# The values of a recurrent mixer leave the projection's front and follow beside the first group's preparation and inversion

## The chip, the cores and the metric

One core of one Trainium2 chip. The metric is the device time of one execution in microseconds (us). The kernel before took 2694.9 us (median of three runs, 2692.5 to 2695.86).

## What is computed

The reference is a trunk of two layers on 256 tokens of width 2048, in float32. Its core for each layer:

```python
mod = (jnp.einsum('bd,de->be', cond, w_ada[l]) + b_ada[l]).reshape(B, N_MOD, 1, D_MODEL)
sh_m, sc_m, gt_m, sh_f, sc_f, gt_f = [mod[:, i] for i in range(N_MOD)]
u = x * (1 + sc_m) + sh_m
proj = u @ w_in[l]                                   # 4896 columns
y_attn = sliding_window_attention(q, k, v, attn_sinks[l], cos, sin)
y_rwkv, v_first = rwkv7_group(proj[..., ATTN_COLS:], ...)
mix = jnp.concatenate([y_attn, y_rwkv], axis=-1) @ w_out[l]
x = layer_norm(DEEPNORM_ALPHA * x + gt_m * mix, ln1_w[l], ln1_b[l])
# then u again with sh_f, sc_f; SwiGLU with 5632 hidden columns; layer_norm
```

Inside `rwkv7_group` the projected columns are 1024 each of r, k and v and 288 low-rank ones (decay, a and gate). Each is mixed with the token before it. From the low-rank ones come the decays w, the rate a and the gate g. In layer 1, v is moved toward layer 0's v (`v_first`) by a gate that is itself computed from v: `v = v + (v_first - v) * sigmoid(v0 + (v @ v1) @ v2)`. Then a state of 64x64 for each of 16 heads runs over the tokens:

```python
S = S * w_t + (S @ a_t) b_t^T + v_t k_t^T     # a = -kk, b = kk * a
out_t = S @ r_t
```

## The kernel before

**Projections.** Weights stream through a pool. `steps` (L363) loads 1024 columns' worth of a weight (`raw`, four buffers, L372), splits them into a rounded part `hi` (ScalarE, L380) and the rest `lo` (VectorE, L381), and each block is three matmuls: hi with the rounded activations, hi with their rest, lo with the rounded ones. `stream` (L402, L403, L405) has tokens on the output's partitions; `tstream` (L414, L415, L416) has the weight's columns there, 128 columns by 256 tokens a matmul. A k-tile is 128 rows of the weight; there are 16. All loads are issued by SyncE (SP) in one order.

**adaLN.** The scales and shifts come from 12 x 2048 columns of `w_ada` a layer, summed by VectorE over 16 rows of k-tiles (L306 for the first scale and shift of layer 0, beside the front; L257 for all others, in the background: `pump()` after each weight step and `adv()` in some places run the next of them). TensorE transposes the sums (L277) and ScalarE adds them up (L281).

**Front.** `front` (L463) runs as soon as parts of the modulated input u are there (`make_u`, L354 to L361). In layer 0 the parts have 4, 4, 2, 4 and 2 k-tiles, and each waits for its part of the first scale and shift. For each part it streams 288 low-rank columns and the 1024 columns of v, and in layer 0 (`ahead`) also 384 of the 512 columns of r and k of the first group: 256 of r, 128 of k. Four accumulators hold v, and in layer 0 a bank that the small products otherwise use holds r.

**Mixer.** `mixer` (L490) first mixes the low-rank columns and all of v with the token before (`shift_mix`, L454, L455); layer 0 stores v, layer 1 loads it and computes the value residual (L523 to L547). The recurrent heads go in four groups of four heads (two pairs), the tokens in four chunks of 64. A string, `ORDER`, one for each layer, gives the order in which the program is written; a scheduler of the framework then sets each engine's order from it. A letter with a group's number stands for:

- D, `decays` (L598 to L625): decays and rates from the low-rank columns; at its end the values are transposed to tokens on partitions (vt, L620).
- R, `project` (L576): r and k of a group. For group 0 of layer 0 only the 128 columns of k that the front left.
- A, `prepare` (L627 to L721): norms (ssb L644, rb L654), the products inside a chunk (aa L681, masked to am L684, stored to DRAM for the inversion L686), the values' product with them (ax L692), at L699, kb L710, and the bonus (bnb L718, bv L720).
- I, `invert` (L723): the inverse of each chunk's unit triangular matrix. Its 16x16 diagonal blocks come back from DRAM (L727), GpSimd (POOL) solves them in 15 steps of two operations (L733, L735), the result goes over DRAM again (L738, L741), and two levels of products follow on TensorE (m, L749 and L756, with VectorE's ytr L745 and yx L752 between).
- C, `recur` (ta L769, tk L775, uv L780, mr L784 and L791, ob, db): the states through the four chunks. E, `close`: normalisation and gate. Q: a third of attention's columns. X changes a pool; a, b, c and w, z are attention and the output projection.

What matters for the order: D, A, I, C of a group follow each other over several engines and DRAM, and the streamed projections R and Q of others are TensorE's work in between.

Of the kernel before, what the change touches and what calls it, by code (L numbers as in the profile page):

```python
# [10 lines left out]
F32 = mybir.dt.float32  # L11
# [8 lines left out]
P = 128  # L20
D = 2048
T = 256
L = 2
KT = D // P
# [4 lines left out]
RW = 1024  # L29
# [12 lines left out]
    "D0 R0 A0 D1 I0 R1 C0 E0 Q1 A1 I1 D2 R2 A2 Q0 D3 C1 R3 E1 I2 A3 X Q2 a0 a1 b0 C2 a2 b1 c0 E2 a3 c1 I3 b2 b3 c2 c3 w0 C3 w1 w2 E3 z0 z1 z2 z3 w3",  # L42
    "D0 R0 A0 D1 R1 I0 C0 Q2 E0 A1 I1 D2 R2 A2 D3 Q1 C1 R3 E1 A3 I2 Q0 X a0 a1 b0 b1 c0 C2 I3 a2 b2 E2 a3 c1 b3 c2 c3 w0 C3 z0 w1 w2 E3 z1 z2 z3 w3",
# [24 lines left out]
def hybrid_trunk_kernel(  # L68
# [19 lines left out]
    turn = [0, 1]  # L88

    def bank(name="mb", tag="mb"):  # L90

        if tag == "cb":
            return ps.tile([P, 512], F32, tag="cb", name=name)
        t = f"m{turn[0]}"
        turn[0] ^= turn[1]
        return ps.tile([P, 512], F32, tag=t, name=name, bufs=1)
# [366 lines left out]
    def front(l, us, feeds, ahead=False):  # L463

        lb = [bank("lb", "cb") for _ in range(2)]
        vb = [acc_ps.tile([P, 512], F32, tag="acc", name="acc") for _ in range(4)]
        lblocks = [(0, 128, lb[0][:, 0:T], True, False), (128, 128, lb[0][:, T:2 * T], False, True),
                   (256, 32, lb[1][0:32, 0:T], not ahead, not ahead)]
        vblocks = [((2 * q + i) * P, P, vb[q][:, i * T:(i + 1) * T], i == 0, i == 1) for q in range(4) for i in range(2)]
        rk = None  # L470
        if ahead:
            b = ps.tile([P, 512], F32, tag="m1", name="rk0", bufs=1)
            turn[:] = 0, 0
            rk = [[b[:, 0:T], b[:, T:2 * T]], [lb[1][:, T:2 * T], None]]
            rblocks = [(0, P, rk[0][0], True, False), (P, P, rk[1][0], True, True), (2 * P, P, rk[0][1], False, True)]
            wrk = w_in[l][:, R0:R0 + 2 * RW].rearrange("(k p) (s n) -> p k s n", p=P, s=2)

            def rk_cols(rv, k0, m):
                return [(rv[:, :, 0:T], wrk[:, k0:k0 + m, 0, 0:T]), (rv[:, :, T:T + P], wrk[:, k0:k0 + m, 1, 0:P])]
        for kts, _ in feeds:  # L480
            fl = dict(first=kts[0] == 0, last=kts[-1] == KT - 1)
            if ahead and kts[0] == 0:
                tstream(rk_cols, T + P, kts, us, rblocks, **fl)
            tstream(cols(w_in[l], LORA0, 288), 288, kts, us, lblocks, **fl)
            if ahead and kts[0] > 0:
                tstream(rk_cols, T + P, kts, us, rblocks, **fl)
            tstream(cols(w_in[l], R0 + 2 * RW, RW), RW, kts, us, vblocks, **fl)
        return lb, vb, rk

    def mixer(l, us, mixp, feeds):  # L490
# [6 lines left out]
        lb, vb, rk = feeds  # L497
        x0 = {}
        if rk:
            for i, s in ((0, 1), (0, 0), (1, 0)):  # L500
                x0[i, s] = pa.tile([P, T], F32, tag=("t_xr", "t_xk")[s], name="x0", bufs=(2, 4)[s])
                shift_mix(l, x0[i, s], rk[i][s], 8 * s + i)
            turn[1] = 1

# [15 lines left out]
        for p in range(NPAIR):  # L520
            shift_mix(l, vx[:, p, :], vb[p // 2][:, p % 2 * T:(p % 2 + 1) * T], 16 + p)
            if l == 0:
                dma(vfirst[p], vx[:, p, :])  # L523
        if l > 0:
# [7 lines left out]
            for p2 in range(4):  # L532
# [3 lines left out]
                for i in range(2):  # L536
                    p = 2 * p2 + i
                    PE.matmul(b[:, i * T:(i + 1) * T], lhsT=v2t[64:96, i * P:(i + 1) * P], rhs=hv, start=True, stop=True)
                for i in range(2):
                    p = 2 * p2 + i  # L540
                    gt = pa.tile([P, T], F32, tag="t_tha", name="gt", bufs=4)
                    S.activation(gt, b[:, i * T:(i + 1) * T], AF.Tanh, scale=0.5, bias=drv(l, "v0h", p))
                    vf = pa.tile([P, T], F32, tag="t_e2", name="vf", bufs=4)
# [6 lines left out]
        left = ["R0", "R1", "R2", "R3", "Q0", "Q1", "Q2"]  # L550
# [19 lines left out]
        wrk = w_in[l][:, R0:R0 + 2 * RW].rearrange("(k p) (s n) -> p k s n", p=P, s=2)  # L570
# [5 lines left out]
        def project(g):  # L576
            if g == 0 and rk:
                b = acc_ps.tile([P, 512], F32, tag="acc", name="acc")
                c0 = R0 + RW + P
                tstream(cols(w_in[l], c0, P), P, list(range(KT)), us, [(0, P, b[:, T:2 * T], True, True)])  # L580
                return [None, b]
            bk = [acc_ps.tile([P, 512], F32, tag="acc", name="acc") for _ in I2]

            def rk_cols(rv, k0, m):
                return [(rv[:, :, s * 256:(s + 1) * 256], wrk[:, k0:k0 + m, s, g * 256:(g + 1) * 256]) for s in range(2)]
            tstream(rk_cols, 512, list(range(KT)), us,
                    [(s * 256 + i * P, P, bk[i][:, s * T:(s + 1) * T], s == 0, s == 1) for i in I2 for s in range(2)])
            return bk

        def decays(g):  # L590
# [26 lines left out]
            vt_ = bank("vt")  # L617
            for cc in range(NCH):
                for i in I2:
                    PE.matmul(vt_[KH[i], cc * P:(cc + 1) * P], lhsT=vx[:, 2 * g + i, cc * CH:(cc + 1) * CH], rhs=cent,  # L620
                              start=True, stop=True)
            for i in I2:
                st[i]["uv"] = uv = pb.tile([P, NCH, P], F32, tag="uv", name="uv", bufs=4)
                S.copy(uv[KH[i]].rearrange("p c s -> p (c s)"), vt_[KH[i]])
            return st  # L625

        def prepare(g, st, bk):  # L627

            nscr = dram.tile([4 * NCH, CH + 1, CH], F32, tag="nscr", name="nscr", bufs=3)
            for i in I2:  # L630
                s_, p = st[i], 2 * g + i
                for s, nm in ((1, "xk"), (0, "xr")):
                    if g == 0 and (i, s) in x0:
                        s_[nm] = x0[i, s]
                    else:
                        s_[nm] = pa.tile([P, T], F32, tag=f"t_{nm}", name=nm, bufs=(2, 4)[s])
                        shift_mix(l, s_[nm], bk[i][:, s * T:(s + 1) * T], 8 * s + p)
# [50 lines left out]
            ax = bank("ax")  # L688
            for cc in range(NCH):
                for h in range(2):  # L690
                    for i in I2:
                        PE.matmul(ax[BH[i], cc * P + h * CH:cc * P + (h + 1) * CH], lhsT=st[i]["am"][h][KH[i], cc, 0:CH],  # L692
                                  rhs=st[i]["uv"][KH[i], cc, h * CH:(h + 1) * CH], start=True, stop=True)
            for i in I2:
                S.copy(st[i]["uv"][BH[i]].rearrange("p c s -> p (c s)"), ax[BH[i]])
# [6 lines left out]
            for i in I2:  # L702
# [9 lines left out]
                S.copy(bkt.rearrange("p c s -> p (c s)"), kb[:, 0:(NCH - 1) * P])  # L712
            bnb = bank("bnb")
# [7 lines left out]
            return nscr  # L721
# [286 lines left out]
        st, bks, nscr = {}, {}, {}  # L1008
# [6 lines left out]
        for op in ORDER[l].split():  # L1015
# [7 lines left out]
            elif op[0] == "A":  # L1023
                nscr[n] = prepare(n, st[n], bks[n])
            elif op[0] == "I":
# [260 lines left out]
    with tc.tile_pool(name="pro", bufs=1) as pp:  # L1286
# [27 lines left out]
        feeds = front(0, us, parts(), ahead=True)  # L1314
# [37 lines left out]
```

## Time and profile before

| what | value |
|---|---|
| median of three runs | 2694.9 us |
| the profiled execution | 2694.28 us |
| its span in the trace | 2692.6 us |
| mean granted TensorE clock | 0.965 |
| TensorE (PE) busy | 2501.1 us, 93% |
| VectorE (DVE) busy | 1841.0 us, 68% |
| ScalarE (ACT) busy | 1188.3 us, 44% |
| GpSimd (POOL) busy | 135.0 us, 5% |
| moved by DMA | 637.49 MB, 237 GB/s on average |

In a row of groups stand: line, engine, operation, out<-in, shapes and count; then the busy time and the mean duration in ns; then the idle time of the engine ahead of these instructions, and who ended it. In a row of the timeline stand the start, the duration, and in brackets the idle time ahead, and who ended it. Matmuls overlap in the pipeline, so their cost in a row of them is the distance between starts. In the table of stretches, each engine's busy time and its number of instructions follow the stretch's length; then come the granted clock, the DMA share and GB/s.

### The profile page before, as it was taken

What the parts mean: (1) busy time and instruction counts of PE and PEld (TensorE: products, weight loads), DVE (VectorE), ACT (ScalarE), POOL (GpSimd) and SP (SyncE); (2) the same over time, 40 slices, a digit from 0 to 9 for tenths busy, and PEclk for the clock granted to TensorE, in tenths of its full rate; (3) what the DMA queues carried; (4) which work ended last, traced back from release to release, by engine and by line L of the source; (5) the groups of instructions that cost most, each with busy time, mean ns of one, the idle gap of its engine ahead of it and who ended that gap; (6) DMA issues with size and microseconds to landing.
All of it is one profiled execution on the core that took longest, in us unless ns stands there. A gap on an engine that the chain in (4) does not pass through costs nothing.

```text
span 2692.6 us, 41752 instructions
## 1 busy us (share of the span) xinstructions
PE 2501.1 (93%) x15325; PEld 2093.1 (78%) x15325; DVE 1841.0 (68%) x2469; ACT 1188.3 (44%) x2029; POOL 135.0 (5%) x355
## 2 busy tenths in 40 slices
PE   3788998788999999999999999979899999999997
PEld 2687886567888888888889877867688888888887
DVE  6866767979877777777788677555764545545456
ACT  2364452435444444444445544534444444344442
POOL 1002112000000000000000022110000000000000
PEclk9789998899999999999999999989999999999999
DMA  9968668688998888889878586424756656666654
GB/s 315 381 188 253 198 191 238 180 317 296 353 330 309 297 303 312 293 295 308 308 263 304 174 259 188 117 72 144 253 172 188 190 186 196 195 189 189 193 188 149
DMA packets 351999, 637.49 MB, mean 237 GB/s; under 512 B 75894, under 2 KB 142898, under 8 KB 350258
## 3 DMA queue, kind: packets, MB, share of 16 engines
q1 hardware_dynamic: 351794, 634.82, 71.6%
q8 instruction: 120, 1.97, 0.3%
q14 instruction: 85, 0.70, 0.1%
HBM read 622.08 MB, written 12.62 MB: 236 GB/s over the span
## 4 chain that ended last, share of the span: by engine, by line
PE 68%; DMA 8%; DVE 6%; ACT 2%; issue 1%; POOL 1%; SPq 0%; DVEq 0%; POOLq 0%; ACTq 0%
PE acc L403 19%; PE acc L402 19%; PE acc L405 19%; DMA ast<-in_w_ada_dram 3%; DVE aacc L257 2%; PE acc L414 2%; PE acc L415 2%; PE acc L416 2%; DVE lo L381 1%; DMA raw<-in_w_gate_up_dram 1%; PE mb L1225 1%; DMA raw<-in_w_out_dram 1%; DMA yf<-yd 1%; PE mb L277 1%; ACT pr L947 0%
## 5 line engine op out<-in xcount | busy, mean ns | idle before, releaser
L380 ACT CAST hi<-raw 128x1024 fp32r<-128x1024 f32 (+2 forms) x728 | 758.5, 1044 | 1110.8 <-PE acc L405 833.1
L381 DVE TENSOR_TENSOR lo<-raw,hi 128x1024 fp32r<-128x1024 f32 (+2 forms) x728 | 880.2, 1212 | 519.8 <-PE acc L403 347.1
L403 PE MATMUL acc<-lo,u 128*128 128x512 f32 x1568 | 513.4, 395 | 11.9 <-DVE lo L381 11.8
L405 PE MATMUL acc<-hi,u 128*128 128x512 f32 x1568 | 505.8, 391 | 0.0
L257 DVE SCALAR_TENSOR_TENSOR aacc<-ast,cond,aacc 128x1024 f32<-128x1024 f32 x300 | 384.1, 1280 | 127.8 <-DMA ast<-in_w_ada_dram 126.6
L402 PE MATMUL acc<-hi,u 128*128 128x512 f32 x1568 | 457.2, 393 | 0.9 <-ACT u L360 0.5
L403 PEld LDWEIGHTS acc<-lo,u 128*128 128x128 f32 x1568 | 293.8, 189 | 76.4 <-DVE lo L381 16.2
L402 PEld LDWEIGHTS acc<-hi,u 128*128 128x128 f32 x1568 | 294.9, 188 | 63.4 <-ACT sg L1218 0.9
L405 PEld LDWEIGHTS acc<-hi,u 128*128 128x128 f32 x1568 | 295.2, 188 | 61.8 <-issue 0.5
L403 PE MATMUL acc<-lo,ht 128*128 128x512 f32 (+1 forms) x720 | 243.6, 377 | 3.0 <-DVE lo L381 2.9
L405 PE MATMUL acc<-hi,ht 128*128 128x512 f32 (+1 forms) x720 | 242.2, 375 | 0.0
L414 PE MATMUL acc<-u,hi 128*128 128x256 f32 x720 | 206.1, 293 | 14.0 <-ACT hi L380 14.0
L402 PE MATMUL acc<-hi,ht 128*128 128x512 f32 (+1 forms) x720 | 217.0, 376 | 0.0
L415 PE MATMUL acc<-u,hi 128*128 128x256 f32 x720 | 204.5, 291 | 0.0
L416 PE MATMUL acc<-u,lo 128*128 128x256 f32 x720 | 193.1, 294 | 7.1 <-DVE lo L381 7.1
L403 PEld LDWEIGHTS acc<-lo,ht 128*128 128x128 f32 x720 | 135.0, 188 | 29.3 <-DVE lo L381 5.6
L414 PEld LDWEIGHTS acc<-u,hi 128*128 128x128 f32 x720 | 141.9, 197 | 19.3 <-ACT hi L380 14.9
L405 PEld LDWEIGHTS acc<-hi,ht 128*128 128x128 f32 x720 | 135.6, 188 | 24.2
L402 PEld LDWEIGHTS acc<-hi,ht 128*128 128x128 f32 x720 | 134.8, 188 | 24.4
L415 PEld LDWEIGHTS acc<-u,hi 128*128 128x128 f32 x720 | 141.7, 197 | 2.6 <-issue 1.6
L416 PEld LDWEIGHTS acc<-u,lo 128*128 128x128 f32 x720 | 133.8, 197 | 11.6 <-DVE lo L381 9.0
L1067 POOL TENSOR_TENSOR brs<-brs,mhalf 128x1 f32<-128x1 f32 x8 | 7.6, 955 | 1698.7 <-DVE brs L1066 772.1
(349 smaller groups left out, 2901.1 us busy)
## 6 DMA issues: line engine op xcount, KB each, us to landing
ast<-in_w_ada_dram SPq DMA_DIRECT2D x368, 512.0 KB
raw<-in_w_gate_up_dram SPq DMA_DIRECT2D x704, 256.0 KB
raw<-in_w_down_dram SPq DMA_DIRECT2D x176, 512.0 KB
raw<-in_w_in_dram SPq DMA_DIRECT2D x82, 512.0 KB
raw<-in_w_out_dram SPq DMA_DIRECT2D x64, 512.0 KB
raw<-in_w_in_dram SPq DMA_DIRECT2D x120, 256.0 KB
ast<-in_w_ada_dram SPq DMA_DIRECT2D x32, 256.0 KB
lnw<-in_ln_w_dram SPq DMA_DIRECT2D x4, 1024.0 KB
```

What stands on the lines that cost most here:

```text
L257: ins = V.scalar_tensor_tensor(acc, t, cond[:, j:j + 1], acc, ALU.mult, ALU.add)
L277: PE.transpose(b[:, i * P:(i + 1) * P], blocks[q + i], ident)
L380: S.copy(h, fl)
L381: ins = V.tensor_tensor(r, fl, h.bitcast(F32), ALU.subtract)
L402: PE.matmul(bt, lhsT=xh, rhs=hi[:, c0:c0 + w], start=st, stop=False)
L403: PE.matmul(bt, lhsT=xh, rhs=lo[:, c0:c0 + w], start=False, stop=False)
L405: PE.matmul(banks[t][q][:, 0:w], lhsT=xl, rhs=hi[:, c0:c0 + w], start=False, stop=sp_)
L414: PE.matmul(bt, lhsT=hi[:, c0:c0 + w], rhs=xh, start=st and opens, stop=False)
L415: PE.matmul(bt, lhsT=hi[:, c0:c0 + w], rhs=xl, start=False, stop=False)
L416: PE.matmul(bt, lhsT=lo[:, c0:c0 + w], rhs=xh, start=False, stop=sp_ and closes)
L1067: G.tensor_tensor(rs[:, 0:1], rs[:, 0:1], mhalf[:, 0:1], ALU.pow)
L1225: PE.transpose(b[:, i * T + t * P:i * T + (t + 1) * P], hh[t][:, (2 * k2 + i) * P:(2 * k2 + i + 1) * P], ident)
```

## The change

The front streams, for each part, the 288 low-rank columns and then the 512 columns of r and k of group 0, in both layers, into two accumulators (`rk_stream`, shared with `project`). The values are streamed by a new step V in two halves of 512 columns each, with their own two accumulators, token mixing and store; in layer 1 the residual follows the second half. What needs the values is taken out of D and A into a new step U, `join`: vt, ax, and the bonus. R0 is gone. The two ORDER strings get V and U; the extra r and k columns' special bank and its handling go. The number of streamed matmuls and the bytes loaded stay the same.

```diff
 ORDER = (
-    "D0 R0 A0 D1 I0 R1 C0 E0 Q1 A1 I1 D2 R2 A2 Q0 D3 C1 R3 E1 I2 A3 X Q2 a0 a1 b0 C2 a2 b1 c0 E2 a3 c1 I3 b2 b3 c2 c3 w0 C3 w1 w2 E3 z0 z1 z2 z3 w3",
-    "D0 R0 A0 D1 R1 I0 C0 Q2 E0 A1 I1 D2 R2 A2 D3 Q1 C1 R3 E1 A3 I2 Q0 X a0 a1 b0 b1 c0 C2 I3 a2 b2 E2 a3 c1 b3 c2 c3 w0 C3 z0 w1 w2 E3 z1 z2 z3 w3",
+    "D0 A0 V0 I0 V1 U0 D1 R1 C0 E0 A1 U1 I1 Q1 D2 R2 A2 U2 D3 C1 R3 E1 I2 Q0 A3 U3 X Q2 a0 a1 b0 C2 a2 b1 c0 E2 a3 c1 I3 b2 b3 c2 c3 w0 C3 w1 w2 E3 z0 z1 z2 z3 w3",
+    "D0 A0 I0 V0 V1 U0 D1 R1 C0 Q2 E0 A1 U1 I1 D2 R2 A2 U2 D3 Q1 C1 R3 E1 A3 U3 I2 Q0 X a0 a1 b0 b1 c0 C2 I3 a2 b2 E2 a3 c1 b3 c2 c3 w0 C3 z0 w1 w2 E3 z1 z2 z3 w3",
 )
...
-    def front(l, us, feeds, ahead=False):
+    def rk_stream(l, g, bk, kts, us, first=True, last=True):
+
+        wrk = w_in[l][:, R0:R0 + 2 * RW].rearrange("(k p) (s n) -> p k s n", p=P, s=2)
...
+        tstream(rk_cols, 512, kts, us,
+                [(s * 256 + i * P, P, bk[i][:, s * T:(s + 1) * T], s == 0, s == 1) for i in range(2) for s in range(2)],
+                first, last)
+
+    def front(l, us, feeds):
...
-        vb = [acc_ps.tile([P, 512], F32, tag="acc", name="acc") for _ in range(4)]
+        bk = [acc_ps.tile([P, 512], F32, tag="acc", name="acc") for _ in range(2)]
...
         for kts, _ in feeds:
             fl = dict(first=kts[0] == 0, last=kts[-1] == KT - 1)
-            if ahead and kts[0] == 0:
-                tstream(rk_cols, T + P, kts, us, rblocks, **fl)
             tstream(cols(w_in[l], LORA0, 288), 288, kts, us, lblocks, **fl)
-            if ahead and kts[0] > 0:
-                tstream(rk_cols, T + P, kts, us, rblocks, **fl)
-            tstream(cols(w_in[l], R0 + 2 * RW, RW), RW, kts, us, vblocks, **fl)
-        return lb, vb, rk
+            rk_stream(l, 0, bk, kts, us, **fl)
+        return lb, bk
...
-        for p in range(NPAIR):
-            shift_mix(l, vx[:, p, :], vb[p // 2][:, p % 2 * T:(p % 2 + 1) * T], 16 + p)
-            if l == 0:
-                dma(vfirst[p], vx[:, p, :])
-        if l > 0:
+
+        def values(half):
+
+            vb = [acc_ps.tile([P, 512], F32, tag="acc", name="acc") for _ in range(2)]
+            tstream(cols(w_in[l], R0 + 2 * RW + half * 512, 512), 512, list(range(KT)), us,
+                    [((2 * q + i) * P, P, vb[q][:, i * T:(i + 1) * T], i == 0, i == 1) for q in range(2) for i in range(2)])
+            for j in range(4):
+                p = 4 * half + j
+                shift_mix(l, vx[:, p, :], vb[j // 2][:, j % 2 * T:(j % 2 + 1) * T], 16 + p)
+                if l == 0:
+                    dma(vfirst[p], vx[:, p, :])
+            if l == 0 or half == 0:
+                return
...
+        def join(g, st):
+
+            vt_ = bank("vt")
...
+            ax = bank("ax")
...
             bnb = bank("bnb")
```

The loops of `join` are those that stood in `decays` and `prepare`, word for word.

**What moves, in three places.** First SP, the end of layer 0's front: before, from its last but two adaLN loads on (`ast`; `raw` is a piece of a weight, 128 partitions by its columns).

```order
L372 DMA raw<-in_w_in_dram 128x2x256
L372 DMA raw<-in_w_in_dram 128x2x128
L301 DMA ast<-in_w_ada_dram 128x2x256 x2
L372 DMA raw<-in_w_in_dram 128x1024 x4
L372 DMA raw<-in_w_in_dram 128x2x288
L372 DMA raw<-in_w_in_dram 128x2x256
L372 DMA raw<-in_w_in_dram 128x2x128
L372 DMA raw<-in_w_in_dram 128x1024 x2
```

And the same place after.

```order
L301 DMA ast<-in_w_ada_dram 128x2x256 x4
L372 DMA raw<-in_w_in_dram 128x2x288
L301 DMA ast<-in_w_ada_dram 128x2x256 x2
L372 DMA raw<-in_w_in_dram 128x2x256 x2
L301 DMA ast<-in_w_ada_dram 128x2x256 x10
L372 DMA raw<-in_w_in_dram 128x2x512 x4
L824 DMA g2a<-in_rwkv_g_dram 128x256
```

Behind the last adaLN load stood the front's weights of the last k-tiles; now all of the front's stand ahead of it, and behind it come the values' first weights (2x512).

Second TensorE, where the first product of layer 0's first inversion (m, 64x64) stands: before, amid `stream`ed projections of attention and group 1's decays (ab).

```order
L403 MATMUL acc<-lo,u 128x512
L405 MATMUL acc<-hi,u 128x512
L402 MATMUL acc<-hi,u 128x512
L599 MATMUL ab<-xwa,w2a_1931 128x256 x2
L402 MATMUL acc<-hi,u 128x512
L749 MATMUL m_2036<-ytr,am 64x64 x16
L403 MATMUL acc<-lo,u 128x512
```

And after.

```order
L415 MATMUL acc<-u,hi 128x256
L695 MATMUL ax<-uv,am 64x64
L416 MATMUL acc<-u,lo 128x256 x2
L695 MATMUL ax<-uv,am 64x64 x8
L734 MATMUL m_1693<-ytr,am 64x64 x16
L695 MATMUL ax<-uv,am 64x64 x7
L704 MATMUL bnb<-xr,bones 128x256
```

The inversion's first product now stands among the values' and the next group's `tstream` (128x256) and the join (ax, bnb), and no longer among attention's projections.

Third TensorE, the last preparation of layer 1: before.

```order
L405 MATMUL acc<-hi,u 128x512
L402 MATMUL acc<-hi,u 128x512
L692 MATMUL ax<-uv,am 64x64 x16
L699 MATMUL at<-ident,ar 64x128 x6
L756 MATMUL m_16858<-tm,yx 64x64 x16
L403 MATMUL acc<-lo,u 128x512
L405 MATMUL acc<-hi,u 128x512
L402 MATMUL acc<-hi,u 128x512
L710 MATMUL kb<-de,bkc 128x128 x3
```

And after.

```order
L655 MATMUL aa<-ar,bkc 128x128 x8
L665 MATMUL at<-ident,ar 64x128 x6
L676 MATMUL kb<-de,bkc 128x128 x6
L686 MATMUL vt<-cent,vx 64x128 x8
L843 MATMUL oc<-ident,sq 128x128 x4
L695 MATMUL ax<-uv,am 64x64 x16
L704 MATMUL bnb<-xr,bones 128x256
L734 MATMUL m_16788<-ytr,am 64x64 x16
L704 MATMUL bnb<-xr,bones 128x256
L741 MATMUL m_16807<-tm,yx 64x64 x16
L734 MATMUL m_16827<-ytr,am 64x64 x16
L891 MATMUL acc<-ident,qr 128x128 x6
```

Before, streamed matmuls (128x512) stood among these products; after, none stands behind the second aa of the last group.

More of the change, by code (lines that the diff above doesn't have):

```diff
@@ L576, in project @@
         def project(g):
[L577 to L581, printed above, removed]
             bk = [acc_ps.tile([P, 512], F32, tag="acc", name="acc") for _ in I2]
[L584 to L587, printed above, removed]
+            rk_stream(l, g, bk, list(range(KT)), us)
             return bk
@@ L616, in decays @@
                 S.activation(e2, lw, AF.Exp, scale=-1.0)
[L617 to L624, printed above, removed]
             return st
```

73 lines of the change are left out of this document (32 added, 41 removed).

## The prediction

> **What bounds the kernel now.** I read the page first: the engine totals, then the forty slices.
>
> ```profile
> span 2692.6 us, 41752 instructions
> PE 2501.1 (93%) x15325; PEld 2093.1 (78%) x15325; DVE 1841.0 (68%) x2469; ACT 1188.3 (44%) x2029; POOL 135.0 (5%) x355
> PE   3788998788999999999999999979899999999997
> ```
>
> TensorE is busy for 93% of the span, so whoever wants to gain must take away TensorE's idle time or its work. The slices show where it idles: at the start, in slices 7 and 8, and in slice 27. The change touches each layer's front and the recurrent mixer behind it, so the next view is the table of stretches: from 40 us to the front's end at about 178 us, layer 0's mixer while it has projections to stream (to 424), and layer 1's front and mixer (1402 to 1661). The columns are PE, weight load, DVE, ACT and POOL busy, the granted clock, the DMA share and GB/s.
>
> ```profile
> 40.00:140.00 100.00, 70.75 (x466) 65.93 (x466) 82.72 (x116) 34.11 (x82) 0.00 (x0) 0.85 1.04 365
> 140.00:178.00 38.00, 35.27 (x268) 33.91 (x270) 22.41 (x34) 21.97 (x43) 0.85 (x3) 0.91 0.51 149
> 178.00:424.00 246.00, 232.65 (x2233) 199.35 (x2230) 179.31 (x272) 123.44 (x247) 41.65 (x103) 0.97 0.71 218
> 1402.00:1479.00 77.00, 71.09 (x562) 68.42 (x560) 62.21 (x89) 42.51 (x67) 1.83 (x4) 0.96 0.79 268
> 1479.00:1661.00 182.00, 168.20 (x1452) 143.24 (x1451) 131.18 (x203) 91.21 (x192) 32.93 (x69) 0.95 0.70 212
> ```
>
> The first 140 us of layer 0 are set by the transfers: their share is 1.04 at 365 GB/s while TensorE has gaps. From 140 on TensorE finishes what the transfers brought late. From 178 on it is TensorE that sets the time, with 246 - 232.65 = 13.35 us of idle time up to 424. Layer 1's front and mixer hold 5.9 and 13.8 us. So in layer 0 a matmul in the front may stand beside transfers for nothing; one in the mixer costs its own time.
>
> **Layer 0's front against its mixer.** The groups of streamed matmuls up to 178 us:
>
> ```profile
> L414 PE MATMUL acc<-u,hi 128*128 128x256 f32 x128 | 37.5, 309 | 14.0 <-ACT hi L380 14.0
> L414 PE MATMUL lb<-u,hi 128*128 128x256 f32 (+1 forms) x64 | 18.4, 318 | 3.7 <-ACT u L360 3.7
> L414 PE MATMUL rk<-u,hi 128*128 128x256 f32 x32 | 10.1, 316 | 1.1 <-ACT u L360 1.1
> 190.05 0.28 PE L415 MATMUL acc<-u,hi 128*128 128x256 f32 x1
> 190.17 0.28 PE L416 MATMUL acc<-u,lo 128*128 128x256 f32 x1
> ```
>
> Each of the three lines of the split has as many: the trace holds 128 + 64 + 32 = 224 per line, 672 in all, or 42 per k-tile (24 values, 9 low-rank, 9 of r and k). One starts every 0.12 us. Behind the front stand another 16 x 3 = 48 for the last k columns. After, the front has 9 + 12 = 21 per k-tile, 336 in all, and 384 of the values stand in the mixer. The 48 are gone, so 384 - 48 = 336 matmuls, 336 x 0.12 = 40.3 us, move from the front to the stretch that TensorE sets. That is +40.3.
>
> What the front gives back: its last modulated input, u, is ready at 147.15 us, behind the last of the adaLN sums on DVE.
>
> ```profile
> 142.87 3.11 DVE L306 SCALAR_TENSOR_TENSOR aacc<-ast,cond,aacc 128x512 f32<-128x512 f32 x4
> 146.73 0.42 DVE L361 TENSOR_TENSOR u<-uf,u 128x256 fp32r<-128x256 f32 x1 [0.41 <-ACT u L360]
> 177.34 0.28 PE L416 MATMUL acc<-u,lo 128*128 128x256 f32 x1
> ```
>
> From there to 177.6 are 30.5 us, which is 6 k-tiles x 42 x 0.12 = 30.2. After, the same six hold 21 each: 15.1 us, so -15.1. And the adaLN loads stand behind fewer weights. Before, the front's raw columns are 1696 x 2048 x 4 = 13.9 MB, of which 3.83 MB (by the shapes of the SP order shown with the change) are issued behind the last adaLN load, so 10.06 MB stand ahead. After, all 800 columns, 6.55 MB, stand ahead. The difference, 3.5 MB at 365 GB/s, is 9.6 us. The front ends 24.7 us earlier (at most 30, if the weights that SP holds back for lack of buffers count too; at least 21, if DVE, 82.72 of 100 us busy, is what held the sums). So this term is 40.3 - 24.7 = **+15.6** (+9 to +19). The front gives back less than the mixer takes, because most of what it loses was hidden beside transfers.
>
> **The front's end.** TensorE waits there for the decays of group 0:
>
> ```profile
> 180.63 0.48 PE L620 MATMUL vt<-cent,vx 128*64 128x128 f32 x2 [1.94 <-ACT lw L605]
> 181.70 0.48 PE L644 MATMUL ssb<-bones,kkn 128*64 128x2 f32 x3 [0.59 <-ACT tha L607]
> 185.26 0.41 PE L414 MATMUL acc<-u,hi 128*128 128x256 f32 x1
> 185.47 0.41 PE L415 MATMUL acc<-u,hi 128*128 128x256 f32 x1
> 1481.38 1.92 PE L530 MATMUL mb<-vx,v1t 128*32 128x256 f32 x4 [2.17 <-DVE vx L455]
> ```
>
> After, the first half of the values stands there with its weights loaded, and vt comes much later. The two waits go, 2.53 us, and the slow steps after them (0.21 against 0.12 us, for some 16 matmuls) cost 1.4: **-3.9** (0 if the values' first scale or weight comes late). In layer 1 the wait of the value residual, 2.17 us, and a like restart (1.4 by layer 0's) go the same way: **-3.5** (0 to -4), since the residual then stands behind the second half, with projections to stream.
>
> **The inversions.** With group 0, TensorE's last product of the preparation (aa) leads over DVE, a DMA round trip and POOL's small triangular solve to the first product of the inversion (m). POOL's first and last row give the length of a solve, here of groups 0 and 1 of layer 0; PE's rows are those at the ends of group 0's chain, and two of layer 1 that wait for DVE.
>
> ```profile
> 215.15 1.49 PE L681 MATMUL aa<-ar,bkc 64*128 64x128 f32 x16
> 254.79 1.44 PE L749 MATMUL m<-ytr,am 64*64 64x64 f32 x22 [6.70 <-DVE ytr L745]
> 1571.48 0.50 PE L403 MATMUL acc<-lo,u 128*128 128x512 f32 x1 [2.20 <-DVE lo L381]
> 1655.39 0.80 PE L403 MATMUL acc<-lo,u 128*128 128x512 f32 x1 [5.32 <-DVE lo L381]
> ```
>
> And POOL's, with the row of DVE beside its second step ahead of them:
>
> ```profile
> 227.54 1.23 DVE L381 TENSOR_TENSOR lo<-raw,hi 128x1024 fp32r<-128x1024 f32 x1
> ```
>
> ```profile
> 226.98 0.72 POOL L733 TENSOR_TENSOR tmp<-nb,ttl 128x15 f32<-128x15 f32 x1 [41.32 <-DMA nb<-nscr]
> 227.78 1.07 POOL L735 TENSOR_TENSOR ttl<-ttl,tmp 128x15 f32<-128x15 f32 x1
> 245.44 0.22 POOL L735 TENSOR_TENSOR ttl<-ttl,tmp 128x8 f32<-128x8 f32 x1
> 297.36 0.21 POOL L733 TENSOR_TENSOR tmp<-nb,ttl 128x15 f32<-128x15 f32 x1 [48.18 <-DMA nb<-nscr]
> 297.65 0.21 POOL L735 TENSOR_TENSOR ttl<-ttl,tmp 128x15 f32<-128x15 f32 x1
> 308.18 0.22 POOL L735 TENSOR_TENSOR ttl<-ttl,tmp 128x8 f32<-128x8 f32 x1
> ```
>
> Group 0's solve takes 18.7 us, its chain from aa's end (216.6) to m 38.2, and m waits 6.70. Group 1's solve, the same steps, takes 11.0, so its chain would be 30.5. In the order after, the work that TensorE has between aa and m is 197, 105, 193 and 134 streamed matmuls and small ones of 4 to 14 us: about 28, 27, 29 and 25 us in the first two inversions of layers 0 and 1. Whether that covers depends on how long the solve gets. With 30.5 everywhere the waits are 2.5, 3.5, 1.5 and 5.5, 13 in all; with 38.2 they are 10, 11, 9 and 13, 43 in all; 6.7 now. I take the first inversion as it is (10) and the short chain in the other three (10.5), which is 13.8 more, and set off the two waits for DVE in layer 1 (2.20 and 5.32) that would fall into them: **+6** (0 to +24).
>
> POOL's step takes 0.21 us at 297.65 and 1.07 at 227.78, beside a DVE row with two inputs (the split lo takes from the weights the cast hi). The Trainium skill ("SBUF — State Buffer", section "SBUF: two separate sides") says that DVE and GpSimd share a port pair under an exclusive lock, held for a whole instruction, when the DVE one has two SBUF inputs. This trace agrees (0.21 against 1.07). By that rule more DVE splits beside each solve mean the long chain in each, and 2742 as in the rival of the long solves below.
>
> **The late mixer.** Layer 0 streams its last projection at 423.6; what follows is the last preparation, bare:
>
> ```profile
> 423.60:443.20 19.60, 15.14 (x186) 12.19 (x185) 11.97 (x16) 5.97 (x16) 3.44 (x14) 0.84 0.86 250
> 428.08 0.44 PE L692 MATMUL ax<-uv,am 64*64 64x64 f32 x6 [1.72 <-DVE am L684]
> 439.29 0.63 PE L277 MATMUL mb<-ident,aacc 128*128 128x128 f32 x4 [2.58 <-DVE aacc L257]
> 1760.07 0.40 PE L405 MATMUL acc<-hi,u 128*128 128x512 f32 x1
> ```
>
> It idles 4.46 us. After, two query projections stand later, beside it: **-4** (-8 to 0). In layer 1 the projections run until 1760 and cover the last preparation today. In the order after, groups 1 to 3 stand later among the streamed matmuls, and the second half of the last preparation, its join and the products of group 2's inversion stand behind the last of them. The same stretch bare cost 4.46 in layer 0: **+5** (0 to +15, if the waits of that inversion are as long as group 0's 6.70 above, twice).
>
> The values' 8.4 MB of weights now stand beside the background adaLN loads; the mixer's share is 0.71, so there is room on average, and I take **+2** (0 to +5) for moments of both. The inversion split in two (what needs the values in a step of its own) adds no instruction.
>
> **Sum.** 15.6 - 3.9 - 3.5 + 6 - 4 + 5 + 2 = +17.2. The profiled execution took 2694.28 us, 1.7 over its span and 0.6 under the median of 2694.9; with it 2694.3 + 17.2 = 2711.5. The bounds above, added as independent (the root of the sum of squares), give -11 and +22, 2700 to 2733 for this case.
>
> **Rivals.** *A wash.* The inversions are covered, the late mixer of layer 1 shows nothing and no transfers crowd: 2694.3 + 15.6 - 3.9 - 3.5 - 4 = 2698.5. For it: group 1 waits for nothing today. Against: less work stands between than today in three of four.
>
> *Faster: the moved matmuls fill idle time.* If the values, free to be streamed at any time, take the place of TensorE's 13.35 idle us in layer 0's mixer and the 13.8 in layer 1's, these fall off instead of the single waits: 2694.3 + 15.6 - 13.35 - 13.8 = 2682.8, 11.5 under now. Against: the idle time is many waits under 3 us for a split or a scale, which a streamed matmul has too. It decides if the stretch behind the front holds under 3 us of idle.
>
> *Long solves.* All four solves take the 18.7 us of group 0: waits of 43 instead of 6.7, +36.4 in place of +6, and 2742. It decides where DVE's splits and adaLN sums fall on most of POOL's steps. For it: the values' splits now stand beside the solves. Against: group 1's 11.0, with DVE working too. (The Trainium skill's lock of the port pair, "SBUF — State Buffer", would lead here.)
>
> *The values' weights starve.* If their stream came slower than 0.12 us a matmul, the front would give its 24.7 and the mixer take more than 40.3; the DMA share of 0.71 says no, and I count it within the range.
>
> **Numbers.** The forecast 0.52, the wash 0.17, the faster case 0.19, the long solves 0.12. Of this kernel a measurement tells about 0.2%, 5.4 us, from no change: the wash lies within that, with some of the forecast's lower end, and a little of the wash is below it. Faster 0.20, the same 0.18, slower 0.62. The range takes in the faster case and the forecast's upper end and leaves out most of the long solves: 2681 to 2736.
>
> **What would show it.** In the profile after, the last streamed matmul of layer 0's front should end near 153 us (177.6 now), and the stretch from there to the last streamed projection should be some 40 us longer. Waits of 2 to 10 us should stand at the first m of the first two inversions. The last preparation in layer 1 should be bare, in layer 0 covered. I am wrong if the front ends before 140, if TensorE's idle time in the two mixers falls by over 15 us, or if POOL's solves last 18 us throughout.

## The result and the profile after

The changed kernel takes 2731.6 us (median of four runs, 2724.1 to 2736.5) beside 2693.7 us before: a ratio of 1.0136, 95% interval 1.0121 to 1.0151. It is slower by 38 us, where 17 were forecast. The profiled execution took 2730.35 us, with a span of 2728.6, 36.0 over that of before.

The page of after, its totals and the slices that answer to those shown:

```profile
span 2728.6 us, 41739 instructions
PE 2507.5 (92%) x15325; PEld 2094.2 (77%) x15325; DVE 1843.4 (68%) x2467; ACT 1186.0 (43%) x2027; POOL 142.1 (5%) x355
PE   2598989788999999999999999978999999999998
```

TensorE's work is the same within 6.4 us; 29.6 of the 36.0 us are idle time. The table of stretches says where. To compare, both kernels are cut at the same streamed matmuls: the end of layer 0's front, the mixer's last streamed projection, the end of the output projection, of the feed-forward part (FFN), and the same three for layer 1. First before, then after, with the columns as in the prediction:

```profile
0.00:177.60 177.60, 108.97 (x743) 101.42 (x743) 129.72 (x189) 62.59 (x144) 10.63 (x66) 0.89 0.90 307
177.60:423.60 246.00, 232.65 (x2232) 199.34 (x2231) 179.38 (x272) 123.53 (x247) 41.65 (x103) 0.97 0.71 218
423.60:635.80 212.20, 175.69 (x1253) 137.28 (x1252) 171.10 (x319) 85.90 (x234) 16.63 (x36) 0.88 0.79 259
635.80:1399.00 763.20, 749.01 (x3478) 619.74 (x3479) 592.60 (x597) 348.85 (x537) 2.45 (x2) 0.99 0.89 307
1399.00:1760.50 361.50, 341.79 (x3116) 298.76 (x3115) 251.84 (x389) 180.99 (x350) 55.09 (x138) 0.97 0.65 201
1760.50:1935.20 174.70, 155.40 (x1104) 121.31 (x1102) 110.57 (x262) 74.74 (x166) 4.66 (x7) 0.91 0.46 151
```

```profile
0.00:151.00 151.00, 66.38 (x409) 58.66 (x409) 109.80 (x167) 43.16 (x119) 10.59 (x66) 0.82 0.92 312
151.00:459.00 308.00, 286.06 (x2637) 248.40 (x2637) 219.55 (x311) 142.82 (x286) 55.58 (x107) 0.97 0.72 221
459.00:660.80 201.80, 168.26 (x1182) 132.54 (x1182) 162.93 (x309) 82.89 (x218) 15.34 (x33) 0.86 0.77 259
660.80:1433.30 772.50, 751.22 (x3478) 619.46 (x3479) 591.19 (x595) 349.30 (x537) 1.06 (x2) 0.99 0.88 302
1433.30:1776.40 343.10, 327.99 (x2865) 288.09 (x2865) 234.23 (x366) 175.81 (x339) 41.01 (x107) 0.97 0.66 201
1776.40:1972.10 195.70, 171.75 (x1357) 133.08 (x1356) 120.16 (x279) 80.69 (x178) 14.77 (x38) 0.92 0.42 136
```

The differences are -26.6, +62.0, -10.4 and +9.3 in layer 0, -18.4 and +21.0 in layer 1, and -0.9 in layer 1's FFN. Layer 0 up to its FFN's end loses 34.3 us, layer 1's two stretches together 2.6. The front is where the trade shows: 42.6 us of TensorE's busy time left it, and it became 26.6 shorter, so its idle time rose from 68.6 to 84.6 us. In the mixer behind it 53.4 us of busy time and 8.6 of idle time came on top.

The front's end, and the two waits at the first inversions in layer 0:

```profile
132.19 0.42 DVE L361 TENSOR_TENSOR u<-uf,u 128x256 fp32r<-128x256 f32 x1
...
140.27 1.53 DVE L306 SCALAR_TENSOR_TENSOR aacc<-ast,cond,aacc 128x512 f32<-128x512 f32 x2
...
145.98 0.42 DVE L361 TENSOR_TENSOR u<-uf,u 128x256 fp32r<-128x256 f32 x1 [1.32 <-ACT u L360]
146.89 0.42 DVE L361 TENSOR_TENSOR u<-uf,u 128x256 fp32r<-128x256 f32 x1 [0.49 <-ACT u L360]
...
220.04 0.69 PE L734 MATMUL m<-ytr,am 64*64 64x64 f32 x8 [6.94 <-DVE ytr L730]
...
321.44 0.59 PE L734 MATMUL m<-ytr,am 64*64 64x64 f32 x6 [5.31 <-DVE ytr L730]
```

The last u, of the fifth part, is made at 146.9 us, when 4 us of the front are left. Before, its like came at 168, when its turn came:

```profile
167.97 0.43 DVE L361 TENSOR_TENSOR u<-uf,u 128x256 fp32r<-128x256 f32 x1 [0.48 <-ACT u L360]
```

The u that the prediction took for the last before (146.73) is the last of the fourth part. Its like comes at 132.19 now, 14.5 us earlier. The last sum of the adaLN columns ends at 141.80, 4.2 us earlier (145.98 before). Both m wait, 12.25 us in all. POOL's solves of those two groups:

```profile
194.87 1.01 POOL L718 TENSOR_TENSOR tmp<-nb,ttl 128x15 f32<-128x15 f32 x1 [24.09 <-DMA nb<-nscr]
195.96 1.12 POOL L720 TENSOR_TENSOR ttl<-ttl,tmp 128x15 f32<-128x15 f32 x1
212.35 0.22 POOL L720 TENSOR_TENSOR ttl<-ttl,tmp 128x8 f32<-128x8 f32 x1
299.26 0.51 POOL L718 TENSOR_TENSOR tmp<-nb,ttl 128x15 f32<-128x15 f32 x1 [7.10 <-DMA nb<-nscr]
299.85 0.28 POOL L720 TENSOR_TENSOR ttl<-ttl,tmp 128x15 f32<-128x15 f32 x1
313.44 0.22 POOL L720 TENSOR_TENSOR ttl<-ttl,tmp 128x8 f32<-128x8 f32 x1
```

They last 17.7 and 14.4 us (18.7 and 11.0 before); those of layer 1's first two groups last 13.5 and 13.2 (15.5 and 16.9). In layer 1 the first two inversions wait little, and a later one, behind the last streamed projection, waits at both of its levels:

```profile
1548.36 0.45 PE L734 MATMUL m<-ytr,am 64*64 64x64 f32 x8 [1.71 <-DVE ytr L730]
1721.14 0.47 PE L734 MATMUL m<-ytr,am 64*64 64x64 f32 x3 [2.78 <-DVE ytr L730]
1795.51 0.77 PE L734 MATMUL m<-ytr,am 64*64 64x64 f32 x12 [4.62 <-DVE ytr L730]
1804.39 0.91 PE L741 MATMUL m<-tm,yx 64*64 64x64 f32 x12 [5.31 <-DVE yx L737]
```

The FFN of layer 0, on which no line was changed, starts with longer waits for its normalised input (5.52 and 1.59 us before):

```profile
667.09 0.69 PE L354 MATMUL mb<-ident,z 128*128 128x128 f32 x2 [6.29 <-DVE z L1067]
670.69 1.12 PE L354 MATMUL mb<-ident,z 128*128 128x128 f32 x4 [2.91 <-DVE z L1067]
```

### The profile page after: what moved, and what is told of

Its sections match the earlier page's. It is cut to its first block, busy times and chain, and to the rows that moved or that the text cites. A ratio compares the mean times of both kernels' runs of the same rounds, so it can differ in the third digit from the quotient of the medians.

```text
span 2728.6 us, 41739 instructions
## 1 busy us (share of the span) xinstructions
PE 2507.5 (92%) x15325; PEld 2094.2 (77%) x15325; DVE 1843.4 (68%) x2467; ACT 1186.0 (43%) x2027; POOL 142.1 (5%) x355
## 5 line engine op out<-in xcount | busy, mean ns | idle before, releaser
L380 ACT CAST hi<-raw 128x1024 fp32r<-128x1024 f32 (+1 forms) x726 | 757.9, 1047 | 1113.3 <-PE acc L405 844.7
L381 DVE TENSOR_TENSOR lo<-raw,hi 128x1024 fp32r<-128x1024 f32 (+1 forms) x726 | 881.1, 1215 | 533.3 <-PE acc L403 364.6
L414 PE MATMUL acc<-u,hi 128*128 128x256 f32 x768 | 220.7, 292 | 0.6 <-ACT hi L380 0.6
L416 PE MATMUL acc<-u,lo 128*128 128x256 f32 x768 | 217.3, 293 | 4.1 <-DVE lo L381 3.9
L415 PE MATMUL acc<-u,hi 128*128 128x256 f32 x768 | 219.6, 289 | 0.0
L416 PEld LDWEIGHTS acc<-u,lo 128*128 128x128 f32 x768 | 146.3, 195 | 12.0 <-DVE lo L381 7.3
L414 PEld LDWEIGHTS acc<-u,hi 128*128 128x128 f32 x768 | 150.1, 196 | 5.3 <-issue 3.0
L415 PEld LDWEIGHTS acc<-u,hi 128*128 128x128 f32 x768 | 150.2, 196 | 2.5 <-issue 1.4
```

The lines of the kernel that those rows point to most:

```text
L380: S.copy(h, fl)
L381: ins = V.tensor_tensor(r, fl, h.bitcast(F32), ALU.subtract)
L414: PE.matmul(bt, lhsT=hi[:, c0:c0 + w], rhs=xh, start=st and opens, stop=False)
L415: PE.matmul(bt, lhsT=hi[:, c0:c0 + w], rhs=xl, start=False, stop=False)
L416: PE.matmul(bt, lhsT=lo[:, c0:c0 + w], rhs=xh, start=False, stop=sp_ and closes)
```

## The experiments

All kernels are built from one source that holds both fronts. `OLD[l]` gives a layer the front, mixer and ORDER of before, `FV[l]` puts half of the values into a layer's changed front; line numbers in their rows are shifted. The scheduler sets the engines' orders anew for each kernel. "The end of layer 0" is the time of the last streamed matmul of its FFN in the profile: 1399.0 us before, 1433.3 after. Ratios are to before, run beside; before's own median was 2693.8 to 2699.1 us in these groups.

**e1: layer 0 alone.**

```diff
-OLD = (0, 0)
+OLD = (0, 1)
```

> Layer 0 as in the changed kernel, layer 1 as before. Theory (layer 0 pays): the profiles put 25.0 us of the loss ahead of layer 0's feed-forward part and 9.3 into that part, where the background adaLN sums stand nine steps further on; both come from layer 0's front, so this kernel takes 2721 to 2730 us. Rival 1 (the 9.3 us are chance, or come from layer 1): 2716 to 2720. Rival 2 (layer 1's late mixer, 21 us longer in the profile, is where the loss arises): below 2712.

Measured: 2726.5 us (2723.2 to 2728.7), ratio 1.0105 (1.0085 to 1.0125). Layer 0 ends at 1432.6, its FFN takes 769.7 us, idle 18.3 (14.2 before):

```profile
662.90:1432.60 769.70, 751.38 (x3479) 620.66 (x3479) 591.67 (x596) 349.21 (x537) 1.06 (x2) 0.99 0.88 303
```

Layer 0 pays, as the theory had it, and most of the FFN's loss comes with layer 0's change. But the two layers' changes don't add up: 1.05% for layer 0 alone and -0.26% for layer 1 alone (e2) make 0.8%, and together they cost 1.36%.

**e2: layer 1 alone.**

```diff
-OLD = (0, 0)
+OLD = (1, 0)
```

> Layer 1 as in the changed kernel, layer 0 as before. Theory (layer 0 pays): layer 1 gives back 18.4 us up to its last streamed projection and takes 21.0 behind it, a shift and no loss: 2694 to 2699 us. Rival 2 (the bare last preparation of layer 1 is a cost of its own): 2705 to 2715.

Measured: 2689.1 us (2681.3 to 2699.4, ten runs), ratio 0.9974 (0.9959 to 0.9989): no loss, even a small gain, below the theory's range. Its profiled execution, 2696.8 us, doesn't show the gain; layer 1's two stretches take 535.8 us there, 536.2 before. The bare end of layer 1's preparations is a shift of work, as was expected.

**e3: half of the values in layer 0's front.**

```diff
             rk_stream(l, 0, bk, kts, us, **fl)
+            if FV[l]:
+                if kts[0] == 0:
+                    vb0 = [acc_ps.tile([P, 512], F32, tag="acc", name="acc") for _ in range(2)]
+                tstream(cols(w_in[l], R0 + 2 * RW, 512), 512, kts, us,
...
```

> The changed kernel, but layer 0's front also streams the first half of the values (33 matmuls a k-tile instead of 21). Theory (a matmul in this front is hidden beside the adaLN loads and sums, but for the last six k-tiles): 192 matmuls, 23.0 us, leave the mixer, and 72 of them, 8.6 us, lengthen the front's end: 14 us faster than the changed kernel, 2713 to 2721 us. Rival (the waits of the inversions are what costs): less streamed work stands between group 0's aa and m, its wait of 6.9 us grows by 3 or more, and the time is 2728 to 2738.

Measured: 2701.6 us (2688.2 to 2708.6), ratio 1.0018 (1.0000 to 1.0036): 30 us better than after, where 14 were expected. The front and the mixer:

```profile
0.00:165.90 165.90, 93.38 (x599) 85.27 (x599) 120.69 (x180) 53.17 (x133) 11.90 (x66) 0.85 0.90 308
165.90:436.90 271.00, 258.82 (x2487) 224.06 (x2488) 197.23 (x290) 132.09 (x261) 49.87 (x133) 0.98 0.72 223
436.90:642.80 205.90, 170.06 (x1141) 133.35 (x1139) 167.89 (x315) 83.04 (x229) 4.42 (x6) 0.85 0.79 260
642.80:1408.40 765.60, 750.03 (x3478) 620.98 (x3479) 590.55 (x593) 350.35 (x537) 2.07 (x2) 0.99 0.88 305
```

The 192 matmuls lengthen the front by 14.9 us, where 8.6 were expected, and shorten the mixer by 37.0. Of the mixer's 37.0 us, 25.5 are these matmuls by the price found below, and 9.8 are idle time, which fell from 21.9 to 12.2. With eight pieces of weight fewer, the mixer also ran fewer of the background sums: 48 by its last streamed projection, and 57 in after (e5 is on these).

**e4: more buffers in layer 0's front.**

```diff
-            raw = wp.tile([P, 1024], F32, tag="raw", name="raw", bufs=WB[0])
+            raw = rawp[0].tile([P, 1024], F32, tag="raw", name="raw", bufs=rawp[1])
...
+        rawp[:] = pp, 8
         feeds = front(0, us, parts())
+        rawp[:] = wp, WB[0]
```

> The changed kernel, but layer 0's front has eight buffers of its own for the pieces of its weights instead of four. Theory (SP's queue: a weight that waits for a buffer holds up the adaLN loads behind it, 8.7 us at the longest, and DVE stands without them from 58 to 66 us): the last u comes 5 to 9 us earlier than 146.9, and the time falls by as much: 2722 to 2727 us. Rival (DVE's sums set the front, busy 80 of 100 us): the last u comes within 2 us of 146.9, and the time stays at 2729 to 2734.

Measured: 2731.7 us (2727.4 to 2743.7), ratio 1.0135 (1.0100 to 1.0171). The time stayed, as the rival had it, but the last u came later, not within 2 us:

```profile
150.82 0.42 DVE L363 TENSOR_TENSOR u<-uf,u 128x256 fp32r<-128x256 f32 x1 [1.33 <-ACT u L362]
151.74 0.42 DVE L363 TENSOR_TENSOR u<-uf,u 128x256 fp32r<-128x256 f32 x1 [0.49 <-ACT u L362]
```

So more buffers for the weights don't bring the front's end forward. The second part's u, too, come at 93.7 us instead of 83.1: with room for more weights these go ahead of the adaLN columns, and the front's end waits for the last of the columns. A side result: throughout layer 0's FFN and layer 1, TensorE's order is the same in this kernel and in after, and DVE's but for one swap. Yet layer 1's two stretches took 531.4 us here and 538.8 in after. Some 7 us of them are thus scatter between executions.

**e5: fewer background sums in layer 0's mixer.**

```diff
-AP = (0.65, 0.3)
+AP = (0.51, 0.3)
```

> The changed kernel, but layer 0's mixer runs 0.51 steps of the background adaLN sums per piece of weight instead of 0.65: the values' 16 pieces gave the mixer 9 to 14 steps more than before. Theory (the sums that run ahead put DVE's and the loads' work onto other places, in layer 0's feed-forward part above all): that part's 772 us fall to 763 to 766, and the kernel takes 2721 to 2726 us. Rival (the feed-forward part's waits have nothing to do with the sums' place): 2729 to 2735.

Measured: 2727.2 us (2724.7 to 2727.5) beside 2699.1 before, ratio 1.0103 (1.0088 to 1.0118), against after's 1.0136: 9 us better by the ratios. Layer 0's mixer, its end and its FFN:

```profile
151.00:447.30 296.30, 283.94 (x2682) 246.37 (x2681) 208.69 (x303) 143.99 (x275) 47.19 (x124) 0.98 0.71 218
447.30:652.40 205.10, 168.58 (x1135) 132.31 (x1135) 160.88 (x306) 80.98 (x213) 8.38 (x16) 0.83 0.74 246
652.40:1417.20 764.80, 749.88 (x3478) 619.75 (x3477) 593.05 (x598) 349.35 (x537) 1.06 (x2) 0.99 0.89 307
```

The FFN takes 764.8, within the theory's 763 to 766, and the mixer is 11.7 us shorter; layer 0 ends at 1417.2, 16.1 earlier than in after. The whole time lies between the two ranges. The trace counts 43 of the background sums' rows on DVE up to the mixer's last streamed projection before, 57 after, and 48 here: `pump()` runs 0.65 steps with every piece of weight, so the values took sums with them into the mixer. Their 16 pieces make some 10 of the 14 more. Layer 1, which now finds the sums further back, took 551.8 us and gave 13.0 of it back. The edit changed more than the sums' place: TensorE's order in layer 0 is another one, too (1135 instructions stand behind the mixer's last streamed projection, and 1182 in after). This run doesn't tell the two apart.

**e6: the split alone, in layer 0.**

```diff
-D0 R0 A0 D1 I0 R1 C0 E0 Q1 A1 I1 D2 R2 A2 Q0 D3 C1 R3 E1 I2 A3 X
+D0 R0 A0 D1 I0 U0 R1 C0 E0 Q1 A1 I1 U1 D2 R2 A2 U2 Q0 D3 C1 R3 E1 I2 A3 U3 X
```

> Layer 0 streams as before (values in the front, 384 columns of r and k ahead), but what needs the values (vt, ax, bonus) is a step of its own behind the inversion, as in the changed kernel; layer 1 as changed. Compare with the kernel that changes layer 1 only (2689.1). Theory (the split itself moves little: the scheduler puts the products where it put them before): 2686 to 2693 us, group 0's m still waits 5 to 8 us. Rival (the split shortens the chain to the inversion): the wait falls below 3 us, 2681 to 2686.

Measured: 2703.1 us (2699.7 to 2706.7) beside 2699.1, ratio 1.0019 (1.0004 to 1.0035), 0.45% above e2. Neither was right: the wait at group 0's m is gone, but one stands at a streamed matmul just ahead of it, and the time is longer. Ahead of the split that this matmul needs (lo), DVE stood still for the load of a background sum:

```profile
248.36 1.28 DVE L260 SCALAR_TENSOR_TENSOR aacc<-ast,cond,aacc 128x1024 f32<-128x1024 f32 x1 [8.38 <-DMA ast<-in_w_ada_dram]
251.22 0.79 PE L406 MATMUL acc<-lo,u 128*128 128x512 f32 x1 [8.89 <-DVE lo L384]
```

The prediction gave the split no price. Here it costs some 12 us by the ratios, of which the two profiled executions show 4.9; no run takes it out of the changed kernel.

**e7: values first, r and k in the mixer.**

```diff
-            return front_old(l, us, feeds, ahead=l == 0)
+            return front_old(l, us, feeds, ahead=False)
```

> Layer 0's front streams the low-rank columns and all values, 33 matmuls a k-tile, and r and k of group 0 wholly in the mixer; split and order as before; layer 1 as changed. The front holds as many matmuls as with half of the values (2701.6), but other ones. Theory (only the number of matmuls that stand beside the front's adaLN loads counts): 2697 to 2706 us. Rival (r and k early start the recurrent chain early, and that is worth something): 2710 to 2720.

Measured: 2724.8 us (2715.1 to 2729.6) beside 2699.1, ratio 1.0092 (1.0069 to 1.0115): the theory fell, and the time lies even above the rival's range. The front is as long as in e3 (164.3 us), but behind the mixer stands a bare recurrence:

```profile
439.40:660.10 220.70, 179.14 (x1245) 138.24 (x1244) 168.40 (x316) 85.60 (x234) 15.67 (x36) 0.82 0.72 240
469.65 0.69 PE L903 MATMUL ob<-state,rh 128*64 128x128 f32 x4 [13.32 <-ACT state L922]
```

This stretch takes 205.9 in e3. So with as many matmuls in the front, but without r and k there, the recurrence is less far on when the projections end, and some 15 us more are taken behind them. How much of this r and k alone make isn't shown: this kernel also has before's ORDER, without the split.

**e8: the first inversion later.**

```diff
-D0 A0 V0 I0 V1 U0 D1 R1 C0
+D0 A0 V0 V1 U0 D1 I0 R1 C0
```

> The changed kernel with layer 0's order 'D0 A0 V0 V1 U0 D1 I0 R1 C0' at the start: both halves of the values, the join and the next decays are written ahead of the inversion, which puts some 3 us more work between aa and m in the first two inversions. Theory (the waits at m, 6.9 and 5.3 us, are lack of work between): both fall by 2 to 3 us, 2723 to 2729 us. Rival (the wait moves on to the recurrence): 2729 to 2735.

Measured: 2714.5 us (2710.6 to 2718.2) beside 2699.1, ratio 1.0058 (1.0043 to 1.0073), better than was expected. But the expected mechanism gives little of it:

```profile
221.00 0.69 PE L840 MATMUL m<-ytr,am 64*64 64x64 f32 x8 [6.42 <-DVE ytr L836]
323.29 0.51 PE L840 MATMUL m<-ytr,am 64*64 64x64 f32 x10 [1.71 <-DVE ytr L836]
1430.30:1951.10 520.80, 492.44 (x4218) 416.33 (x4216) 355.64 (x644) 256.28 (x517) 55.19 (x145) 0.96 0.59 184
```

The waits fell by 0.5 and 3.6 us and layer 0 ends 3.0 earlier. Layer 1's two stretches fell by 18.0, though only layer 0's ORDER was edited: the scheduler put layer 1's last recurrence and the output projection in another order.

**e9: before, with the sums drawn forward.**

```diff
-AP = (0.65, 0.3)
+AP = (0.93, 0.3)
```

> The kernel before with one number changed: layer 0's mixer runs 0.93 steps of the background adaLN sums per piece of weight instead of 0.65, so that they stand as far on at its end as in the changed kernel. Theory (the sums drawn forward cost up to 16 us in layer 0 by themselves, as the kernel with 0.51 showed the other way round): up to the end of layer 0, 1399.0 us in the profile before, it takes 8 to 18 us more. Rival (the sums' place costs only beside the moved values): within 4 us of 1399, and the time within 4 us of before.

Measured: 2712.4 us (2709.3 to 2713.7) beside 2693.8, ratio 1.0063 (1.0045 to 1.0082). Layer 0 ends at 1426.3, 27.3 us later than before: more than the theory's 8 to 18, and in another place, the stretch behind the mixer, where it takes 235.7 us for 212.2:

```profile
425.40:661.10 235.70, 186.35 (x1310) 147.29 (x1310) 186.23 (x342) 85.64 (x222) 16.00 (x36) 0.80 0.76 249
```

So drawing the sums forward costs without any moved value, too. It drew more forward than the change did: by the end of the output projection 112 sums had run, 98 before and 107 in after. Here, too, TensorE's order changed with it (1310 instructions in that stretch, 1253 before). The whole time grew by only 18.6 us, as layer 1 took 8.4 less.

**e10: later inversion and fewer sums together.** `AP = (0.51, 0.3)`, e8's ORDER, and in the FFN `AF_ = (0.79, 0.55)` for 0.75.

> The changed kernel with the later inversion of layer 0 and with 0.51 steps in its mixer; its feed-forward part runs 0.79 instead of 0.75, so that layer 1 finds the sums where it did in the changed kernel. Theory (the sums' place and the waits at the inversion are separate): the end of layer 0, 1433.3 us in the changed kernel and 1417.2 with the pace alone, comes at 1410 to 1416, still 11 or more behind before's 1399.0, since the moved matmuls cost 45 and the front gives 27; whole time 1.000 to 1.006 of before. Rival (without the sums' place nothing is left of the loss): 1396 to 1404.

Measured: 2721.5 us (2714.8 to 2726.2) beside 2693.8, ratio 1.0097 (1.0072 to 1.0122); layer 0 ends at 1422.3, behind both ranges. The two don't add up: 5 us later than with the pace alone. That a loss is left with fewer sums holds (23 us here, 18 in e5).

**e11: half of the values in the front, later inversion, as many sums as before.** `FV = (1, 0)`, e8's ORDER, `AP = (0.58, 0.3)`.

> Half of the values in layer 0's front, the later inversion, and 0.58 steps of the sums per piece in its mixer (as many steps in all as before); layer 1 as changed. Theory (144 moved matmuls cost 19 us, the front gives 12, and the recurrence's earlier start gives some back): layer 0 ends at 1396 to 1406, and the time lies 0.994 to 1.001 of before. Rival (each half of the moved values costs alike, half of the 18 us with the pace alone): layer 0 ends at 1406 to 1412.

Measured: 2686.7 us (2680.2 to 2692.4, ten runs) beside 2693.8, ratio 0.9969 (0.9955 to 0.9983): faster than both kernels, and within the theory's range. Layer 0:

```profile
0.00:163.30 163.30, 87.72 (x599) 80.03 (x599) 120.83 (x180) 53.10 (x133) 9.53 (x66) 0.87 0.91 313
163.30:431.40 268.10, 255.18 (x2450) 220.18 (x2450) 196.36 (x289) 131.47 (x259) 41.43 (x112) 0.99 0.75 226
431.40:631.50 200.10, 169.02 (x1175) 133.33 (x1175) 160.99 (x307) 81.71 (x215) 11.82 (x28) 0.86 0.75 252
```

Front and mixer take 7.8 us more than before, the stretch behind them 12.1 less, and layer 0 ends at 1397.6. But e2, with layer 0 as before, has nearly the same ratio, 0.9974 (0.9959 to 0.9989): that this layer 0 gains over that of before isn't shown.

**e12: the same layer 0, with layer 1 of before.** `OLD = (0, 1)` in e11.

> Layer 0 as in the run with half of the values in its front, the later inversion and 0.58 steps; layer 1 as before. Theory (layer 1's part of the change is a shift that costs and gains nothing): as with layer 1 changed, 0.994 to 0.9995 of before. Rival (layer 1's part is what gained in the runs that beat before, 0.26% there): 0.9995 to 1.003.

Measured: 2706.4 us (2701.8 to 2713.1) beside 2695.8, ratio 1.0039 (1.0024 to 1.0055): neither range holds it. Layer 0 ends at 1394.8, 4.2 ahead of before, and layer 1 gives it all back:

```profile
1394.80:1954.10 559.30, 514.42 (x4226) 434.06 (x4225) 365.91 (x653) 260.55 (x533) 57.45 (x145) 0.92 0.57 178
```

These 559.3 us are 536.2 in the kernel before, of the same source. What the sums' place and the scheduler's order each do to layer 1 isn't told apart by these runs.

## Why the prediction was right in direction and wrong in size

**Layer 0's front: right in size, by luck in part.** -24.7 was forecast and -26.6 measured. The prediction took the fourth part's last u for the last. It came 14.5 us earlier, where 9.6 was forecast. From there to the front's end it was to be 15.1 us less; it was 12.0 less (18.4 for 30.5). The last adaLN sum, which the 9.6 stood for, came only 4.2 earlier. So the two errors nearly cancel. What counts is the idle time: it grew by 16.0 us. TensorE's waits for the adaLN columns' sums came to 48.4 us in the front, and to 5.3 before: the values had been its work beside them. (The term's lower bound should be +10 by its own figures, 40.3 - 30, and not +9; that moves the range by under 1 us.)

**The moved matmuls: mis-priced.** The 336 were priced at 0.12 us, their distance when nothing is between. Added up over the mixer's rows, from start to start (without waits), a `tstream` matmul took 82.1 us / 624 = 0.132 before and 127.7 / 958 = 0.133 after, while the median distance was 0.120 in both: the slow stretches behind waits and the small products are in the mean. The 334 more in that stretch cost 45.6, not 40.3. The stretch was to be some 40 us longer and was 62.0; beside the 45.6, 8.6 are idle time, and most of the rest is small work that stood behind the cut before.

**The inversions: right.** 10 and 3.5 us of waits were forecast for layer 0, and 6.9 and 5.3 came. Layer 1's were 1.7 and 2.8 (1.5 and 5.5 forecast). POOL's steps without a DVE instruction beside them took 0.21 to 0.26 us (128 of 240), and each one over 0.36 us stood beside a DVE instruction with two inputs or more. The solves did not all get long, though: of the four, one stayed near its length, one grew and layer 1's two shrank, and the four waits came to 16.7 us, far under the 43 of the rival of the long solves. By the Trainium skill's rule on the port pair that was weighed in the prediction ("SBUF — State Buffer", section "SBUF: two separate sides") all four solves could have been long; the steps agree with the rule, the four lengths don't.

**The late mixers.** Layer 0's was given -4 and showed -10.4, of which 7.4 us is work of TensorE that now stands ahead of the cut. Layer 1 was given +1 in all (-3.5, +5, and -0.5 of the inversions) and showed +2.6: the sum was right, though it comes from a shift of about 20 us past the cut that the terms did not foresee in size. The +5 had the mechanism: a later inversion's waits of 4.62 and 5.31 us stand there. With some 7 us of scatter in layer 1 (e4), so close an agreement is in part luck.

**The step that failed** is the one on the values' loads: "+2 (0 to +5) for moments of both". It asked whether two streams of loads fit beside each other, and they do (a share of 0.72). It put at nothing that each piece of weight also runs 0.65 steps of the background sums. With the values' 16 pieces, 57 sums instead of 43 had run by the end of layer 0's mixer, and DVE's work there and in the FFN stood elsewhere. No term and no rival held this. Layer 0 lost 34.3 us, against 14.5 from the sum's terms for it (15.6 - 3.9 - 4, and 6.8 of the inversions). With the pace set back (e5) it lost 18.2, which is 16.1 less; drawing the sums forward in the kernel before (e9) cost 27.3 there. Less of it shows in the whole time, 9 us in e5 and 18.6 in e9, as layer 1 moved the other way.

How the sums come to cost this isn't shown. TensorE's idle time in layer 0 behind the front that falls into DVE's sums, or into DVE's waits for their loads, is about 19 us before and after alike, so they don't hold TensorE up directly. And the order of the instructions changed with the pace in e5 and in e9. Order alone can be worth as much: in e8, with the pace as it was, layer 1 took 18.0 us less.

What stays open is layer 1's size. It took 520.8 to 559.3 us in these kernels, and about 7 us of that is scatter. So e5 still lost 28 us in all by its ratio, where 17 were forecast.

## What to carry to other kernels

Where a phase is set by loads and sums, matmuls beside them cost less than their own time, and moving them out gains less: here 42.6 us of TensorE's work left the front, which became 26.6 shorter, and cost 45.6 where TensorE sets the time. What starts a long chain is worth having early in such a phase: without r and k there, the recurrence stood bare for some 15 us more (with another order, so this isn't a price). Filler that fits beside the loads is better left there: with half of the values back in the front the loss was nearly gone, though the sums moved with them. That this beats the kernel before isn't shown, as changing layer 1 alone gained as much. And count every hook that hangs on a step that is moved: the background work that it drives moves too.

## What was not expected of the hardware

POOL's small steps took 0.21 to 0.26 us alone and mostly 1.0 to 1.3 where a DVE instruction with two inputs held them up, in both kernels, so a solve of the same 30 operations ranged from 10.2 to 19.5 us. And with the same order of instructions on TensorE, and but for one swap on DVE, executions of two kernels differed by 7 us in one layer's mixer and attention.
